# A hybrid decoder layer: small joint products placed one by one between the large ones, and two of seven sums formed by TensorE

## The chip, the cores and the metric

The kernel runs on one core of one Trainium2 chip. The metric is the device time of one execution in microseconds (us), as the median of several runs. The core has five engines with their own queues, each strictly in the order in which its instructions were issued: TensorE (PE, matmuls; PEld are its weight loads), VectorE (DVE), ScalarE (ACT), GpSimd (POOL) and SyncE (SP, which here only starts transfers). PE writes its results into PSUM, which has eight banks of 128 x 512 float32; DVE and ACT read it, POOL does not.

## What is computed

One layer on 1024 tokens of width 1024, all in float32:

```python
def _hybrid_layer(x, norm_g, w_in, ...):
    h = _rmsnorm(x, norm_g)
    p = h @ w_in                      # 1024 x 1024 times 1024 x 6656
    (u, v, z_a, x_b, b_g, c_g, z_b, x_c, z_c, g_a, g_b, g_c) = jnp.split(p, _split_points(), axis=-1)
    y_a = (_gmlp_branch(u, v, ln_g, ln_b, w_s, b_s) * jax.nn.silu(z_a)) @ w_pa
    y_b = (_shortconv_branch(x_b, b_g, c_g, conv_w, conv_b) * jax.nn.silu(z_b)) @ w_pb
    y_c = (_pool_branch(x_c, w_pool, pool_scale) * jax.nn.silu(z_c)) @ w_pc
    merged = jax.nn.sigmoid(g_a) * y_a + jax.nn.sigmoid(g_b) * y_b + jax.nn.sigmoid(g_c) * y_c
    return x + merged @ w_o
```

and a final RMSNorm over the result. The change lies in `h @ w_in`.

## The kernel before

There are three stages. The first (to 76 us) normalises and transposes x, forms its sums and does the columns of v. The middle stage (76 to 632 us) does the other 56 column tiles of `w_in`, two at a time: 28 pairs, `for p, (kind, j, _) in enumerate(pairs)`. The last one does the branch projections, the merge and the output product.

**Products.** A pair of column tiles (B, 2 x 2 blocks of weights) against the activations (A, 2 x 2 blocks) is done with seven block products instead of eight (Strassen's scheme in Winograd's form). `PRODUCTS` numbers them 0 to 6: A11·B11, A12·B21, S2·T2, S3·T3, S1·T1, A22·T4, S4·B22, with sums S of A and T of B. Each float32 operand is cut into a high and a low part, so `mm3` issues three matmuls for each of four 128-row blocks: 12 matmuls of 128 x 512 for one large product. The results are combined by seven sums: with P0 copied to `s1` by ACT, `o0` low half = P0 + P1, `u2` = P2 + s1, `u3` = P3 + u2, `o1` high half = P4 + u3, `u2` = P4 + u2, `o0` high half = P5 + u3, `o1` low half = P6 + u2. All are DVE adds; `block` does those that form a result and the activation behind them.

**Joint products.** From pair 2 on (`PLAIN = 2`), product 1 of an even pair and of the odd one behind it are taken together and done by the same scheme one level down, as seven small products of six matmuls of 128 x 256. `joint(d0, d1)` does all seven ahead of the even pair, in the order `SUB_ORDER`, with one ACT copy and seven DVE adds of 128 x 256 into two buffers `p2`; each pair then adds its `p2` to P0. So a large pair has six products from there on, (0, 2, 3, 4, 5, 6). Their A sums (`*_again`) are made once, in `cut_again`.

**Order.** `steps` lists all products in the order of the code. `product()` takes the next step, calls `ahead`, which prepares the weights (T sums, the cut into high and low by ACT and DVE or POOL) of up to six steps ahead and starts loads up to twelve ahead, and then issues the matmuls into a new PSUM bank. A framework places waits and buffers: tiles of one tag share a fixed number of buffers (PSUM 8; `raw` 4; `q` 6 for p2, s1, u2, u3 and others; `m` 5 for o0, o1 and the buffers of the branches; `wc` 18 for weights). When the program is built it also fixes each engine's order of instructions, which need not be that of the code.

**Kinds of pairs.** The order of kinds is g g g a g a g a g a, then four times b bz, then four times c g, then g g. Gates (g) get a sigmoid and are stored from ACT's queue. For each a pair, `spatial` loads `vr` during the pair before, `spatial_norm` scales it (eight DVE instructions, line 445, two POOL multiplications, a cut), `spatial_mm` uses it in the a pair, and `gate` runs in the pair behind (`late`). Behind a b pair, DVE runs a convolution of three passes; behind a c pair it runs `pooled`, a chain of up to five passes over 128 x 1024 and a cut.

Line 76 is the helper `tt` (every two-operand DVE or POOL instruction), lines 79 and 80 the cut, lines 83 to 85 `mm3`, line 546 the copy to `s1`.

Of the kernel before, what the change touches and what calls it, by code (L numbers as in the profile page):

```python
# [11 lines left out]
ALU = mybir.AluOpType  # L12

P = 128
# [9 lines left out]
HALF = 512  # L24
# [17 lines left out]

PRODUCTS = (("A11", "B11"), ("A12", "B21"), ("S2", "T2"), ("S3", "T3"),
            ("S1", "T1"), ("A22", "T4"), ("S4", "B22"))
BLOCKS = ("A11", "A12", "A22", "S1", "S2", "S3", "S4")
SUB_ORDER = (0, 2, 1, 3, 4, 5, 6)
PLAIN = 2
AHEAD = 6  # L50
RAW_AHEAD = 12
# [4 lines left out]
def hybrid_layer(ctx: ExitStack, tc: tile.TileContext, x, units, ws, wpool, small, rows, out):  # L56
    nc = tc.nc
# [8 lines left out]
    def slot(tag, name, shape, dtype=F32):  # L66
        return big.tile(list(shape), dtype, name=name, tag=tag, bufs=BUFS[tag])

    def bank(name, shape=(P, HALF)):
        return psum.tile(list(shape), F32, name=name, tag="ps")  # L70

    def tsl(i, n=P):
        return slice(i * n, (i + 1) * n)

    def tt(eng, o, a, b, op):
        eng.tensor_tensor(out=o, in0=a, in1=b, op=op)  # L76
# [2 lines left out]
        nc.scalar.copy(out=hi, in_=src)  # L79
        tt(eng or nc.vector, lo, src, hi.bitcast(F32), ALU.subtract)  # L80

    def mm3(ps, wh, wl, bh, bl, first, last):
        nc.tensor.matmul(ps, lhsT=wh, rhs=bh, start=first, stop=False)  # L83
        nc.tensor.matmul(ps, lhsT=wh, rhs=bl, start=False, stop=False)  # L84
        nc.tensor.matmul(ps, lhsT=wl, rhs=bh, start=False, stop=last)  # L85

    tmp = const.tile([P, 3, 3, NT], F32, name="tmp")

# [76 lines left out]
    hb = {}  # L165
# [95 lines left out]
    pairs = []  # L261
# [11 lines left out]


    steps = []
    for p in range(len(pairs)):
        if p < PLAIN:
            steps += [("n", p, r) for r in range(7)]
        else:
            if p % 2 == 0:  # L280
                steps += [("j", p, r) for r in SUB_ORDER]
            steps += [("n", p, r) for r in (0, 2, 3, 4, 5, 6)]
    NP = len(steps)

    raw, T, comb = {}, {}, {}
# [6 lines left out]
    def prep(n):  # L292
        kind, p, r = steps[n]
        name = PRODUCTS[r][1]
        u0, u1 = pairs[p][2]
        load_raw(u0)
        if kind == "n":
            load_raw(u1)
            b = {"B11": raw[u0][:, 0, :], "B21": raw[u0][:, 1, :], "B12": raw[u1][:, 0, :], "B22": raw[u1][:, 1, :]}
        else:  # L300
            v0 = pairs[p + 1][2][0]
            load_raw(v0)
            b = {"B11": raw[u0][:, 1, 0:256], "B21": raw[u0][:, 1, 256:], "B12": raw[v0][:, 1, 0:256],
                 "B22": raw[v0][:, 1, 256:]}

        def add(name, i0, i1, into=None):
            if kind == "n":
                t = bank(f"{name}_{kind}{p}")
            else:
                t = slot("T", f"{name}_{kind}{p}", (P, HALF)) if into is None else into  # L310
            if kind == "j" and into is None:
                T[kind, p, name, "rest"] = t[:, 256:]
                t = t[:, 0:256]
            tt(nc.vector if kind == "n" else nc.gpsimd, t, b[i0] if i0 in b else T[kind, p, i0], b[i1] if i1 in b else T[kind, p, i1], ALU.subtract)
            T[kind, p, name] = t

        if r == 2:
            add("T1", "B12", "B11")
            add("T2", "B22", "T1", T["j", p, "T1", "rest"] if kind == "j" else None)
        elif r == 3:  # L320
            add("T3", "B22", "B12")
        elif r == 5:
            add("T4", "B21", "T2", T["j", p, "T3", "rest"] if kind == "j" else None)
        if kind == "n":
            hi = slot("wc", f"ch{n}", (P, HALF), F32R)
            lo = slot("wc", f"cl{n}", (P, HALF), F32R)
            if name in b:
                split_to(hi, lo, b[name], nc.gpsimd)
            else:
                split_to(hi, lo, T[kind, p, name])  # L330
            comb[n] = (hi, lo)
        elif r == 0:
            hi = slot("wc", f"ch{n}", (P, HALF), F32R)
            lo = slot("wc", f"cl{n}", (P, HALF), F32R)
            split_to(hi, lo, raw[u0][:, 1, :])
            comb[n] = (hi[:, 0:256], lo[:, 0:256])
            comb[n + SUB_ORDER.index(1)] = (hi[:, 256:], lo[:, 256:])
        elif r > 1:
            w = slot("wc", f"cj{n}", (P, 2, 256), F32R)
            split_to(w[:, 0, :], w[:, 1, :], b[name] if name in b else T[kind, p, name])  # L340
            comb[n] = (w[:, 0, :], w[:, 1, :])
# [13 lines left out]
    at_step = [0]  # L355
    sub = {}

    def product():
        n = at_step[0]
        at_step[0] += 1  # L360
        ahead(n)
        kind, p, r = steps[n]
        wh, wl = comb.pop(n)
        if kind == "n":
            ah, al = hb[PRODUCTS[r][0]]
            ps = bank(f"p{n}")
        else:
            ah, al = sub[PRODUCTS[r][0]]
            ps = bank(f"p{n}", (P, 256))
        nk = KH if kind == "n" else KH // 2  # L370
        for k in range(nk):
            mm3(ps, wh[:, tsl(k)], wl[:, tsl(k)], ah[:, k, :], al[:, k, :], k == 0, k == nk - 1)
        return ps

    def cut_again(first):
# [21 lines left out]
            sub["S4"] = sub["A21"]  # L397
            split_to(*sub["S4"], sub["f"])

    def joint(d0, d1):  # L400

        lo, hi = slice(0, 256), slice(256, HALF)
        nc.scalar.copy(out=d0[:, lo], in_=product())
        tt(nc.vector, d1[:, lo], product(), d0[:, lo], ALU.add)
        tt(nc.vector, d0[:, lo], product(), d0[:, lo], ALU.add)
        tt(nc.vector, d0[:, hi], product(), d1[:, lo], ALU.add)
        ps = product()
        tt(nc.vector, d1[:, hi], ps, d0[:, hi], ALU.add)
        tt(nc.vector, d1[:, lo], ps, d1[:, lo], ALU.add)
        tt(nc.vector, d0[:, hi], product(), d0[:, hi], ALU.add)  # L410
        tt(nc.vector, d1[:, lo], product(), d1[:, lo], ALU.add)


    for n, i in enumerate(TOKENS):
# [8 lines left out]
    gates = [dram.tile([P, S], F32, name=f"gate{n}") for n in range(24)]  # L423
# [3 lines left out]
    def spatial(j):  # L427
        both = slot("q", f"wsr{j}", (P, 4, P))
        wsr, lnr = both[:, 0:2, :], both[:, 2:4, :]
        nc.scalar.dma_start(out=wsr, in_=ws[:, 2 * j:2 * j + 2, :])  # L430
        nc.gpsimd.affine_select(out=wsr, in_=wsr, pattern=[[0, 2], [1, P]], compare_op=ALU.is_ge, fill=0.0,
                                base=0, channel_multiplier=-1)
        wss = slot("q", f"wss{j}", (P, 2, 2 * P), F32R)
        src = wsr.rearrange("p g t -> p (g t)")
        split_to(wss[:, 0, :], wss[:, 1, :], src)
        for r in range(2):
            lo = r * CW + j * P
            nc.scalar.dma_start(out=lnr[:, r, :], in_=rows[0:1, lo:lo + P].broadcast_to([P, P]))
# [72 lines left out]
    lohalf, hihalf = slice(0, HALF), slice(HALF, S)  # L511
# [5 lines left out]
    for p, (kind, j, _) in enumerate(pairs):  # L517
        nxt = pairs[p + 1] if p + 1 < len(pairs) else (None, None)
        f0, f1 = FUNCS[kind]
        o0 = slot("m", f"o0_{p}", (P, S))  # L520
        o1 = slot("m", f"o1_{p}", (P, S))
# [12 lines left out]
            elif func:  # L534
                nc.scalar.activation(out=dst, in_=dst, func=func)

        if p >= PLAIN and p % 2 == 0:
            p2, p2_next = (slot("q", f"p2_{p + e}", (P, HALF)) for e in range(2))
            joint(p2, p2_next)
        elif p >= PLAIN:  # L540
            p2 = p2_next
        s1 = slot("q", f"s1_{p}", (P, HALF))
        u2 = slot("q", f"u2_{p}", (P, HALF))
        u3 = slot("q", f"u3_{p}", (P, HALF))
        ps = product()
        nc.scalar.copy(out=s1, in_=ps)
        if nxt[0] == "a":
            sp_next = spatial(nxt[1])
        if p < PLAIN:
            block(o0, lohalf, product(), s1, f0)  # L550
        else:
            block(o0, lohalf, ps, p2, f0)
        if p == PLAIN - 1:
            cut_again(False)
        tt(nc.vector, u2, product(), s1, ALU.add)
        tt(nc.vector, u3, product(), u2, ALU.add)
        if nxt[0] == "a":
            sp_next = spatial_norm(nxt[1], *sp_next)
        if p == 0:
            cut_again(True)  # L560
        ps = product()
        block(o1, hihalf, ps, u3, f1)
        tt(nc.vector, u2, ps, u2, ALU.add)
        block(o0, hihalf, product(), u3, f0)
        if kind == "a":
            st = spatial_mm(j, *sp)
        sp = sp_next
        if late is not None:
            late()
            late = None  # L570
        if kind == "g":
            nc.scalar.dma_start(out=gates[2 * j], in_=o0)
        block(o1, lohalf, product(), u2, f1)

        if kind == "g":
            nc.scalar.dma_start(out=gates[2 * j + 1], in_=o1)
# [131 lines left out]
    for b in range(3):  # L708
        for e, d in enumerate(ORDER):
            n = 8 * b + e  # L710
# [10 lines left out]
            wh, wl = wps.pop(n)  # L721
            py = [bank(f"py{n}_{h}") for h in range(2)]
            for c in range(CT):
                for w, s in ((wh, 0), (wh, 1), (wl, 0)):
                    for h in range(2):
                        nc.tensor.matmul(py[h], lhsT=w[:, tsl(c)], rhs=yt[b][h][s][:, c, :],  # L726
                                         start=c == 0 and w is wh and s == 0, stop=c == CT - 1 and w is wl)
# [188 lines left out]
```

## Time and profile before

| | |
|---|---|
| median of 3 runs | 864.05 us (864.03 to 864.22) |
| the profiled execution | 864.74 us |
| its span, first to last instruction | 863.0 us |
| mean granted TensorE clock | 0.984 of full speed |
| PE busy | 826.1 us (96%) |
| DVE busy | 661.5 us (77%) |
| ACT busy | 341.2 us (40%) |
| POOL busy | 373.5 us (43%) |

A line of a timeline or of a group names source line, engine, operation, "out<-in" by the program's tile names without numbers (`p` is a bank of a product, but also a `p2` buffer; `T_n` a T sum of a large product, `ch`/`cl` and `cj` cut weights, `o` a result, `u` one of u2 and u3, `s` is s1, `pl` and `pw` belong to `pooled`), and the shape. In brackets stands the idle time of the engine in front of the instruction and what ended it. Matmuls overlap: each takes 0.39 us from start to end at 512 columns, but the next starts before that.

### The profile page before, as it was taken

To read this page: it belongs to the slowest core of one execution; us is meant where nothing else is said; L and a number is where in the kernel's file an instruction comes from. 1 tells how busy PE (TensorE), PEld (TensorE's weight loads), DVE (VectorE), ACT (ScalarE), POOL (GpSimd) and SP (SyncE) were. 2 spreads that over 40 slices of the span, in tenths; PEclk is the share of its full clock that TensorE was granted. 3 is DMA by queue.
4 is the path that set the end of the run, shared out by engine and by line. 5 is a ranking of instruction groups with operands and counts; after the bars stand their busy time and mean duration, and the time that the engine had idled before them with its cause. 6 is when DMAs were issued, how large, how long until landed. Compare 5 with 4: busy or idle time off the path is not lost.

```text
span 863.0 us, 11355 instructions
## 1 busy us (share of the span) xinstructions
PE 826.1 (96%) x3950; PEld 694.5 (80%) x3950; DVE 661.5 (77%) x1102; ACT 341.2 (40%) x667; POOL 373.5 (43%) x347
## 2 busy tenths in 40 slices
PE   7999999898989999999999999999999999997993
PEld 6787888787878888888888888888888888775883
DVE  6867887878787878869686787879565735897995
ACT  4545444444444433323234453535342401343431
POOL 5743535646464624354351213141000352548874
PEclk8999999999999999999999999999999999999997
DMA  7412332323323212031121413323498553421044
GB/s 293 159 38 74 119 124 88 110 98 93 116 85 123 74 49 98 25 118 65 62 94 32 150 73 102 119 80 123 147 333 301 171 171 122 147 74 50 11 161 146
DMA packets 33880, 99.57 MB, mean 115 GB/s; under 512 B 3488, under 2 KB 9632, under 8 KB 33824
## 3 DMA queue, kind: packets, MB, share of 16 engines
q1 hardware_dynamic: 27920, 83.90, 28.2%
q10 hardware_dynamic: 5904, 14.96, 4.9%
q8 instruction: 31, 0.51, 0.2%
q14 instruction: 25, 0.20, 0.1%
HBM read 73.68 MB, written 25.17 MB: 115 GB/s over the span
## 4 chain that ended last, share of the span: by engine, by line
PE 78%; DVE 11%; DMA 3%; POOL 3%; issue 2%; ACT 1%; POOLq 0%; DVEq 0%; ACTq 0%
PE p L83 20%; PE p L85 20%; PE p L84 20%; PE py L726 10%; DVE al L76 3%; PE pv L85 2%; PE pv L83 2%; DVE rq L76 2%; PE pv L84 2%; POOL res L76 1%; DVE mg L76 1%; POOL S_a L76 1%; DVE vr L445 1%; DVE gt L76 1%; DMA out_dram<-res 1%
## 5 line engine op out<-in xcount | busy, mean ns | idle before, releaser
L76 POOL TENSOR_TENSOR cl<-raw,ch 128x512 fp32r<-128x512 f32 x58 | 79.8, 1378 | 230.7 <-ACT ch L79 105.3
L79 ACT CAST ch<-T_n 128x512 fp32r<-128x512 f32 x112 | 64.7, 587 | 116.7 <-PE p L84 61.3
L76 DVE TENSOR_TENSOR o<-p,u 128x512 f32<-128x512 f32 x84 | 57.7, 687 | 43.2 <-PE p L85 42.7
L76 DVE TENSOR_TENSOR cl<-T_n,ch 128x512 fp32r<-128x512 f32 x112 | 75.5, 679 | 7.2 <-ACT ch L79 6.8
L79 ACT CAST ch<-raw 128x512 fp32r<-128x512 f32 x71 | 43.7, 620 | 70.4 <-PE p L84 59.5
L76 DVE TENSOR_TENSOR u<-p,u 128x512 f32<-128x512 f32 x56 | 38.3, 683 | 10.6 <-PE p L85 9.6
L83 PE MATMUL p<-A11h,ch 128*128 128x512 f32 x112 | 44.3, 396 | 0.3 <-ACT ch L79 0.3
L85 PE MATMUL p<-A11h,cl 128*128 128x512 f32 x112 | 43.7, 390 | 0.6 <-POOL cl L76 0.6
L83 PE MATMUL p<-S4h,ch 128*128 128x512 f32 x112 | 43.9, 392 | 0.0
L84 PE MATMUL p<-A11l,ch 128*128 128x512 f32 x112 | 43.8, 391 | 0.0
L85 PE MATMUL p<-S4h,cl 128*128 128x512 f32 x112 | 43.6, 389 | 0.0
L84 PE MATMUL p<-S4l,ch 128*128 128x512 f32 x112 | 43.6, 389 | 0.0
L85 PE MATMUL p<-A22h,cl 128*128 128x512 f32 x112 | 43.6, 389 | 0.0
L83 PE MATMUL p<-S2h,ch 128*128 128x512 f32 x112 | 43.6, 389 | 0.0
L84 PE MATMUL p<-S2l,ch 128*128 128x512 f32 x112 | 43.6, 389 | 0.0
L85 PE MATMUL p<-S2h,cl 128*128 128x512 f32 x112 | 43.6, 389 | 0.0
L83 PE MATMUL p<-S3h,ch 128*128 128x512 f32 x112 | 43.6, 389 | 0.0
L84 PE MATMUL p<-S3l,ch 128*128 128x512 f32 x112 | 43.6, 389 | 0.0
L85 PE MATMUL p<-S3h,cl 128*128 128x512 f32 x112 | 43.6, 389 | 0.0
L83 PE MATMUL p<-S1h,ch 128*128 128x512 f32 x112 | 43.6, 389 | 0.0
L84 PE MATMUL p<-S1l,ch 128*128 128x512 f32 x112 | 43.6, 389 | 0.0
L85 PE MATMUL p<-S1h,cl 128*128 128x512 f32 x112 | 43.6, 389 | 0.0
(475 smaller groups left out, 2533.0 us busy)
## 6 DMA issues: line engine op xcount, KB each, us to landing
raw<-in_units_dram SPq DMA_DIRECT2D x56, 512.0 KB, 3.3
gate<-o ACTq DMA_DIRECT2D x24, 512.0 KB, 3.1
gt<-gate SPq DMA_DIRECT2D x24, 512.0 KB, 4.5
rawp<-in_units_dram SPq DMA_DIRECT2D x12, 512.0 KB, 3.6
yr<-y SPq DMA_DIRECT2D x12, 512.0 KB, 4.8
x<-in_x_dram SPq DMA_DIRECT2D x8, 512.0 KB, 6.7
y<-o SPq DMA_DIRECT2D x8, 512.0 KB, 2.6
rawo<-in_units_dram SPq DMA_DIRECT2D x8, 512.0 KB, 3.3
```

The costliest lines, as they stand in the source:

```text
L76: eng.tensor_tensor(out=o, in0=a, in1=b, op=op)
L79: nc.scalar.copy(out=hi, in_=src)
L83: nc.tensor.matmul(ps, lhsT=wh, rhs=bh, start=first, stop=False)
L84: nc.tensor.matmul(ps, lhsT=wh, rhs=bl, start=False, stop=False)
L85: nc.tensor.matmul(ps, lhsT=wl, rhs=bh, start=False, stop=last)
L445: nc.vector.tensor_scalar(out=vr[:, i, :], in0=vr[:, i, :], scalar1=mv[:, i, 0:1], scalar2=lr[:, i:i + 1], op0=ALU.subtract, op1=ALU.mult)
L726: nc.tensor.matmul(py[h], lhsT=w[:, tsl(c)], rhs=yt[b][h][s][:, c, :], start=c == 0 and w is wh and s == 0, stop=c == CT - 1 and w is wl)
```

## The change

Six things change.

1. The seven small products are no longer done in a row ahead of an even pair. `subs_behind` puts them behind large products: in the odd pair before, one behind product 3, two behind product 5, one behind product 6; in the even pair, one each behind products 0, 4 and 2. Their order becomes 0, 2, 1, 3, 5, 4, 6. `joint(q, r)` now does one of them; `then` is called behind each large product and does those that stand next in `steps`.
2. The large products go in the order 0, 4, 2, 3, 5, 6 (`ORDER_N`; pairs 0 and 1 have product 1 behind 0). T1 is formed for product 4.
3. Product 2 is accumulated onto the bank of product 0 (`px`) after `o0 <- P0 + p2` has read it. ACT copies P0+P2 to `u2`; `s1` is gone (pairs 0 and 1 also copy P0).
4. Product 6 is accumulated onto the bank of product 4 (`py_`) after `o1 <- P4 + u3` has read it; the second `u2` add is gone. In the same way the small product 6 goes onto the bank of the small product 4.
5. `spatial_norm` and `cut_again(True)` stand behind `o1 <- P4 + u3` instead of ahead of it.
6. The store of a gate's `o0` stands right behind its last half instead of behind the late work.

```diff
 BLOCKS = ("A11", "A12", "A22", "S1", "S2", "S3", "S4")
-SUB_ORDER = (0, 2, 1, 3, 4, 5, 6)
+ORDER_N = (0, 4, 2, 3, 5, 6)
+SUB_ORDER = (0, 2, 1, 3, 5, 4, 6)
+SUB_BEFORE = {3: 1, 5: 2, 6: 1}
+SUB_WITHIN = {0: 1, 4: 1, 2: 1}
...
     steps = []
+    subs = {p: list(SUB_ORDER) for p in range(PLAIN, len(pairs), 2)}
+    def subs_behind(p, r):
+        q = p + p % 2
+        at = SUB_BEFORE if p % 2 else SUB_WITHIN
+        return q, [subs[q].pop(0) for _ in range(at.get(r, 0))] if q in subs else []
     for p in range(len(pairs)):
-        if p < PLAIN:
-            steps += [("n", p, r) for r in range(7)]
-        else:
-            if p % 2 == 0:
-                steps += [("j", p, r) for r in SUB_ORDER]
-            steps += [("n", p, r) for r in (0, 2, 3, 4, 5, 6)]
+        for r in ((0, 1) + ORDER_N[1:] if p < PLAIN else ORDER_N):
+            steps.append(("n", p, r))
+            q, rs = subs_behind(p, r)
+            steps += [("j", q, e) for e in rs]
...
-        if r == 2:
+        if r == 4 and kind == "n":
             add("T1", "B12", "B11")
+        elif r == 2:
+            if kind == "j":
+                add("T1", "B12", "B11")
             add("T2", "B22", "T1", T["j", p, "T1", "rest"] if kind == "j" else None)
...
-    def product():
+    def product(want, onto=None, more=False):
...
+        ps = bank(f"p{n}", (P, HALF) if kind == "n" else (P, 256)) if onto is None else onto
         nk = KH if kind == "n" else KH // 2
         for k in range(nk):
-            mm3(ps, wh[:, tsl(k)], wl[:, tsl(k)], ah[:, k, :], al[:, k, :], k == 0, k == nk - 1)
+            mm3(ps, wh[:, tsl(k)], wl[:, tsl(k)], ah[:, k, :], al[:, k, :], k == 0 and onto is None,
+                k == nk - 1, more or onto is not None)
...
-    def joint(d0, d1):
+    def joint(q, r):
         lo, hi = slice(0, 256), slice(256, HALF)
-        nc.scalar.copy(out=d0[:, lo], in_=product())
-        tt(nc.vector, d1[:, lo], product(), d0[:, lo], ALU.add)
-        tt(nc.vector, d0[:, lo], product(), d0[:, lo], ALU.add)
-        tt(nc.vector, d0[:, hi], product(), d1[:, lo], ALU.add)
-        ps = product()
-        tt(nc.vector, d1[:, hi], ps, d0[:, hi], ALU.add)
-        tt(nc.vector, d1[:, lo], ps, d1[:, lo], ALU.add)
-        tt(nc.vector, d0[:, hi], product(), d0[:, hi], ALU.add)
-        tt(nc.vector, d1[:, lo], product(), d1[:, lo], ALU.add)
+        if r == 0:
+            for e in range(2):
+                both[q + e] = slot("q", f"p2_{q + e}", (P, HALF))
+        d0, d1 = both[q], both[q + 1]
+        if r == 4:
+            held[q] = product(("j", r), more=True)
+            tt(nc.vector, d1[:, hi], held[q], d1[:, hi], ALU.add)
+        elif r == 6:
+            tt(nc.vector, d1[:, lo], product(("j", r), held[q]), d1[:, lo], ALU.add)
+        elif r == 0:
+            nc.scalar.copy(out=d0[:, lo], in_=product(("j", r)))
+        else:
+            d, part = {2: (d1[:, lo], d0[:, lo]), 1: (d0[:, lo], d0[:, lo]), 3: (d1[:, hi], d1[:, lo]),
+                       5: (d0[:, hi], d1[:, hi])}[r]
+            tt(nc.vector, d, product(("j", r)), part, ALU.add)
...
-        s1 = slot("q", f"s1_{p}", (P, HALF))
...
-        ps = product()
-        nc.scalar.copy(out=s1, in_=ps)
+        px = product(("n", 0), more=True)
         if nxt[0] == "a":
             sp_next = spatial(nxt[1])
+        then(0)
         if p < PLAIN:
-            block(o0, lohalf, product(), s1, f0)
+            nc.scalar.copy(out=u2, in_=px)
+            block(o0, lohalf, product(("n", 1)), u2, f0)
...
         else:
-            block(o0, lohalf, ps, p2, f0)
...
-        tt(nc.vector, u2, product(), s1, ALU.add)
-        tt(nc.vector, u3, product(), u2, ALU.add)
-        if nxt[0] == "a":
-            sp_next = spatial_norm(nxt[1], *sp_next)
-        if p == 0:
-            cut_again(True)
-        ps = product()
-        block(o1, hihalf, ps, u3, f1)
-        tt(nc.vector, u2, ps, u2, ALU.add)
-        block(o0, hihalf, product(), u3, f0)
+            block(o0, lohalf, px, both[p], f0)
+        py_ = product(("n", 4), more=True)
+        then(4)
+        nc.scalar.copy(out=u2, in_=product(("n", 2), px))
+        then(2)
+        tt(nc.vector, u3, product(("n", 3)), u2, ALU.add)
+        block(o1, hihalf, py_, u3, f1)
+        then(3)
+        if p == 0:
+            cut_again(True)
+        if nxt[0] == "a":
+            sp_next = spatial_norm(nxt[1], *sp_next)
+        block(o0, hihalf, product(("n", 5)), u3, f0)
+        if kind == "g":
+            nc.scalar.dma_start(out=gates[2 * j], in_=o0)
+        then(5)
         if kind == "a":
             st = spatial_mm(j, *sp)
...
-        if kind == "g":
-            nc.scalar.dma_start(out=gates[2 * j], in_=o0)
-        block(o1, lohalf, product(), u2, f1)
+        block(o1, lohalf, product(("n", 6), py_), u2, f1)
+        then(6)
```

## Rows read from the trace of the kernel before

**Rows 1.** The page: busy time, share of the span and instructions of each engine

```profile
PE 826.1 (96%) x3950; PEld 694.5 (80%) x3950; DVE 661.5 (77%) x1102; ACT 341.2 (40%) x667; POOL 373.5 (43%) x347
```

**Rows 2.** Waits of PE, 76 to 632 us: in total, times, longest

```profile
PE p L83 <- DVE cl L76: 5.6, 3, 1.9
PE p L83 <- DVE o L76: 2.1, 3, 0.7
```

**Rows 3.** Windows: length, busy (instructions) of PE, PEld, DVE, ACT, POOL, clock, DMA

```profile
115.10:120.10 5.00, 5.00 (x43) 4.98 (x42) 5.00 (x12) 3.41 (x7) 0.00 (x0) 1.00 0.50 185
154.10:162.20 8.10, 5.56 (x44) 5.11 (x43) 7.08 (x16) 2.62 (x5) 4.77 (x3) 1.00 0.08 25
197.10:206.40 9.30, 6.75 (x44) 6.31 (x43) 8.25 (x19) 3.73 (x7) 5.00 (x3) 0.85 0.09 26
241.70:250.90 9.20, 6.66 (x43) 6.24 (x42) 8.26 (x18) 3.64 (x7) 5.00 (x3) 0.84 0.07 17
...
251.00:632.00 381.00, 381.00 (x1866) 323.31 (x1866) 298.03 (x480) 154.01 (x276) 131.97 (x107) 1.00 0.27 95
```

**Rows 4.** Timeline of DVE in the joint group at 154 us: start, us, instruction

```profile
155.59 0.54 DVE L445 TENSOR_SCALAR vr<-vr,mv,lr 128x128 f32<-128x128 f32 x1 [1.02 <-DMA vr<-v_dram]
...
157.76 2.31 DVE L445 TENSOR_SCALAR vr<-vr,mv,lr 128x128 f32<-128x128 f32 x5
```

**Rows 5.** Timeline of PE in the same group

```profile
157.89 0.39 PE L83 MATMUL p<-S1h_again,cj 128*128 128x256 f32 x1 [0.69 <-DVE o L76]
...
160.72 0.39 PE L83 MATMUL p<-A12h,cj 128*128 128x256 f32 x1 [1.85 <-DVE cl L76]
```

**Rows 6.** Groups by form, 76 to 632 us: count, busy us, mean ns, idle before

```profile
L76 DVE TENSOR_TENSOR u<-p,u 128x512 f32<-128x512 f32 x56 | 38.3, 683 | 10.6 <-PE p L85 9.6 <-POOL T_j L76 0.9
...
L76 DVE TENSOR_TENSOR p<-p,p 128x256 f32<-128x256 f32 x91 | 34.6, 410 | 0.0
...
L76 DVE TENSOR_TENSOR u<-p,s 128x512 f32<-128x512 f32 x28 | 19.2, 685 | 10.7 <-PE p L85 10.7
L76 DVE TENSOR_TENSOR o<-p,p 128x512 f32<-128x512 f32 x26 | 17.7, 682 | 5.0 <-ACT s L546 4.8
L546 ACT COPY s<-p 128x512 f32<-128x512 f32 x28 | 16.3, 581 | 0.4 <-PE p L85 0.4
```

**Rows 7.** Timeline of PE in pair 0, from product 1 on

```profile
79.75 0.39 PE L83 MATMUL p<-A12h,ch 128*128 128x512 f32 x1
...
80.21 0.39 PE L83 MATMUL p<-S2h,ch 128*128 128x512 f32 x1
...
82.70 0.39 PE L83 MATMUL p<-A12h,ch 128*128 128x512 f32 x1
```

**Rows 8.** Timeline of PE: first matmul of product 0 in pairs 11, 21, 23, 25

```profile
308.41 0.39 PE L83 MATMUL p<-A11h,ch 128*128 128x512 f32 x1
498.43 0.39 PE L83 MATMUL p<-A11h,ch 128*128 128x512 f32 x1
537.49 0.39 PE L83 MATMUL p<-A11h,ch 128*128 128x512 f32 x1
576.55 0.39 PE L83 MATMUL p<-A11h,ch 128*128 128x512 f32 x1
```

**Rows 9.** Timeline of DVE: the add `o0 <- P0 + p2` of these pairs, and neighbours

```profile
313.98 0.68 DVE L76 TENSOR_TENSOR o<-p,p 128x512 f32<-128x512 f32 x1
504.76 0.68 DVE L76 TENSOR_TENSOR o<-p,p 128x512 f32<-128x512 f32 x1
545.62 0.68 DVE L76 TENSOR_TENSOR o<-p,p 128x512 f32<-128x512 f32 x1
583.17 0.68 DVE L76 TENSOR_TENSOR u<-p,s 128x512 f32<-128x512 f32 x1
585.77 1.23 DVE L76 TENSOR_TENSOR pw<-pl,ph 128x1024 fp32r<-128x1024 f32 x1 [0.17 <-ACT ph L79]
586.91 0.68 DVE L76 TENSOR_TENSOR o<-p,p 128x512 f32<-128x512 f32 x1
```

More of the change, by code (lines that the diff above doesn't have):

```diff
@@ L80, in split_to, with mm3 @@
         tt(eng or nc.vector, lo, src, hi.bitcast(F32), ALU.subtract)
[L82 to L85, printed above, removed]
+    def mm3(ps, wh, wl, bh, bl, first, last, shared=False):
+        nc.tensor.matmul(ps, lhsT=wh, rhs=bh, start=first, stop=False, skip_group_check=shared)
+        nc.tensor.matmul(ps, lhsT=wh, rhs=bl, start=False, stop=False, skip_group_check=shared)
+        nc.tensor.matmul(ps, lhsT=wl, rhs=bh, start=False, stop=last, skip_group_check=shared)
     tmp = const.tile([P, 3, 3, NT], F32, name="tmp")
@@ L336, in prep @@
             comb[n] = (hi[:, 0:256], lo[:, 0:256])
-            comb[n + SUB_ORDER.index(1)] = (hi[:, 256:], lo[:, 256:])
+            comb[steps.index(("j", p, 1))] = (hi[:, 256:], lo[:, 256:])
         elif r > 1:
@@ L362, in product @@
         kind, p, r = steps[n]
+        assert (kind, r) == want
         wh, wl = comb.pop(n)
[L364 to L369, printed above, removed]
+        ah, al = (hb if kind == "n" else sub)[PRODUCTS[r][0]]
+        ps = bank(f"p{n}", (P, HALF) if kind == "n" else (P, 256)) if onto is None else onto
         nk = KH if kind == "n" else KH // 2
         for k in range(nk):
-            mm3(ps, wh[:, tsl(k)], wl[:, tsl(k)], ah[:, k, :], al[:, k, :], k == 0, k == nk - 1)
+            mm3(ps, wh[:, tsl(k)], wl[:, tsl(k)], ah[:, k, :], al[:, k, :], k == 0 and onto is None,
+                k == nk - 1, more or onto is not None)
         return ps
@@ L398, in cut_again @@
             split_to(*sub["S4"], sub["f"])
-    def joint(d0, d1):
+    both, held = {}, {}
+    def joint(q, r):
         lo, hi = slice(0, 256), slice(256, HALF)
-        nc.scalar.copy(out=d0[:, lo], in_=product())
-        tt(nc.vector, d1[:, lo], product(), d0[:, lo], ALU.add)
-        tt(nc.vector, d0[:, lo], product(), d0[:, lo], ALU.add)
-        tt(nc.vector, d0[:, hi], product(), d1[:, lo], ALU.add)
-        ps = product()
-        tt(nc.vector, d1[:, hi], ps, d0[:, hi], ALU.add)
-        tt(nc.vector, d1[:, lo], ps, d1[:, lo], ALU.add)
-        tt(nc.vector, d0[:, hi], product(), d0[:, hi], ALU.add)
-        tt(nc.vector, d1[:, lo], product(), d1[:, lo], ALU.add)
+        if r == 0:
[13 more added lines that the diff above has]
+            tt(nc.vector, d, product(("j", r)), part, ALU.add)
     for n, i in enumerate(TOKENS):
@@ L535, in block, with then @@
                 nc.scalar.activation(out=dst, in_=dst, func=func)
[L537 to L541, printed above, removed]
-        s1 = slot("q", f"s1_{p}", (P, HALF))
+        def then(r):
+            while at_step[0] < NP and steps[at_step[0]][0] == "j":
+                joint(steps[at_step[0]][1], steps[at_step[0]][2])
         u2 = slot("q", f"u2_{p}", (P, HALF))
         u3 = slot("q", f"u3_{p}", (P, HALF))
-        ps = product()
-        nc.scalar.copy(out=s1, in_=ps)
+        px = product(("n", 0), more=True)
         if nxt[0] == "a":
             sp_next = spatial(nxt[1])
+        then(0)
         if p < PLAIN:
-            block(o0, lohalf, product(), s1, f0)
-        else:
-            block(o0, lohalf, ps, p2, f0)
-        if p == PLAIN - 1:
-            cut_again(False)
-        tt(nc.vector, u2, product(), s1, ALU.add)
-        tt(nc.vector, u3, product(), u2, ALU.add)
+            nc.scalar.copy(out=u2, in_=px)
+            block(o0, lohalf, product(("n", 1)), u2, f0)
+            if p == PLAIN - 1:
+                cut_again(False)
+        else:
+            block(o0, lohalf, px, both[p], f0)
[8 more added lines that the diff above has]
+            cut_again(True)
         if nxt[0] == "a":
             sp_next = spatial_norm(nxt[1], *sp_next)
-        if p == 0:
-            cut_again(True)
-        ps = product()
-        block(o1, hihalf, ps, u3, f1)
-        tt(nc.vector, u2, ps, u2, ALU.add)
-        block(o0, hihalf, product(), u3, f0)
+        block(o0, hihalf, product(("n", 5)), u3, f0)
+        if kind == "g":
+            nc.scalar.dma_start(out=gates[2 * j], in_=o0)
+        then(5)
         if kind == "a":
```

## The prediction

> **What bounds the kernel now.** I read the page first: TensorE (PE) is busy for 826.1 of 863.0 us, VectorE (DVE) for 661.5 [rows 1]. That alone says "PE-bound", so the next question is where PE is *not* busy, and only the middle stage (76 to 632 us, the 28 pairs) is touched by the change. The waits of PE there are few: three on a DVE subtraction, three on a DVE add [rows 2]. The windows show where: from 251 us to 632 us PE is busy for 381.00 of 381.00 us at clock 1.00, whereas three of the thirteen groups of small joint products have holes [rows 3]. A clean group takes 5.0 us from its first small product to the large one behind it; the groups at 154, 197 and 242 us take 8.1, 9.3 and 9.2. In each PE idles 2.54 or 2.55 us, and in the last two the granted clock is below 1.00 (0.85 and 0.84 of the window; part of it at the 1.2 GHz level) behind the idle time. So what the change can win is 3.1 + 4.3 + 4.2 = 11.6 us, 1.3% of the span. Everything else that it takes from DVE has no place on the path.
>
> Why those three? DVE sits 1.02 us in front of its queue's first `vr` scaling, waiting for a load, and then does five more in one go (2.31 us) [rows 4]. Meanwhile seven small products come in 5 us, each wanting a PSUM bank and an add; PE then stops first behind an add and then behind a subtraction that reads a bank [rows 5]: the banks are all waiting for DVE.
>
> **The change, part by part.**
> *Sums on TensorE.* Per pair the adds `u2 = P2 + s1` and `u2 = P4 + u2` go: 28 of 0.685 us and half of the 56 of 0.683 us; per joint group one of 0.410 us goes, 13 in all [rows 6]. That is 19.2 + 19.1 + 5.3 = 43.6 us of DVE, off the path while PE has no gap: worth nothing by itself outside the three groups. PE runs as many matmuls of the same shapes as before, so its own work costs 0. The ACT copy of P0 (0.581 us [rows 6]) becomes a copy of P0+P2; two copies more in pairs 0 and 1, beside PE work: 0.
>
> *Small products spread.* Seven in a row become runs of one or two. A run of one or two asks for as many banks and adds in the 2.7 us of the large product next to it, instead of seven in 5.0 us; the demand that filled the banks in [rows 5] is gone. I take all 11.6 us as won, and 0 as the other end. Next late is DVE's wait for `vr` itself: it is still there (1.02 us), see the second rival.
>
> *Order inside a pair* (0, 4, 2, 3, 5, 6). T1 is formed at the same second place as before, T2 one place later; both are DVE adds off the path, 0. Holding P0 and P4 in banks longer takes one or two more of the eight, while T1 and T2 are held for one product less each: I set these against each other. The new argument of `mm3` issues nothing.
>
> *New wait one: product 2 goes onto the bank that the add `o0 <- P0 + p2` reads.* Its first matmul waits for that add, and behind it in PE's queue wait all later products. A large product is 12 matmuls of 0.227 us (two take 79.75 to 80.21 [rows 7]), 2.72 us. In an odd pair only product 4 stands between, so product 2 is due 24 × 0.227 = 5.44 us after product 0 starts; in an even pair two small ones more, 6.9 us. Before, nobody waited for this add, and the trace shows when it came. After a pooling pair (odd pairs 19, 21, 23, 25) it comes behind the pooling chain (in pair 25 right behind its last pass, `pw` at 585.77 [rows 9]): product 0 starts at 498.43, 537.49 and 576.55 [rows 8], so product 2 would be due at 503.87, 542.93 and 581.99; the adds end at 504.76 + 0.68 = 505.44, 546.30 and 587.60 [rows 9]. Lateness 1.6, 3.4 and 5.6 us (pair 19: none). After a convolution pair (11, 13, 15, 17) 308.41 + 5.44 = 313.85 against 313.98 + 0.68 = 314.66: 0.8 us, four times alike. The other odd pairs and the even ones have room. Upper end: 1.6 + 3.4 + 5.6 + 4 × 0.8 = 13.8 us; lower end 0.
>
> Which value? At the four convolution pairs the add had to come behind ACT's copy of the same bank (4.8 us of its idle time over the run are ACT's [rows 6]), and that copy is gone: 0. At pair 25 the `u2` and `u3` adds stood between (0.6 us each by their starts, `u2` at 583.17 ahead of `o0` at 586.91 [rows 9]); those come later now, so 5.6 becomes 4.4. The order on PE is fixed when the program is built, and not strictly by the code: at 79.75 two matmuls of A12 are issued, then ten of S2, then A12 again [rows 7]. So I expect one other ready product, 2.72 us, to be put in front of the waiting one. That leaves 0, 0.7 and 1.7 us: 2.4 us. Without it, 9.4.
> The Trainium skill ("TensorE: Matmul & The Clock Gate", Part 2) says that matmuls themselves stay in program order on the chip and only weight loads are pulled ahead. By that the queue cannot help itself, and the sum for these pairs would be 9.4 us if the issue order isn't changed beforehand; the interleaving in [rows 7] can then only be an issue order.
>
> *New wait two: product 6 goes onto the bank of P4*, read by `o1 <- P4 + u3`. The two adds (0.68 each) follow product 3, and product 5 (2.72 us) runs meanwhile: 1.2 us to spare in even pairs, 3.3 in odd ones, where three small products lie between. `spatial_norm` (8 DVE scalings, 2 POOL products, a cast, a subtraction; no DMA) is moved behind this add, so it stands in front of the next pair's work rather than of this add: 0. The 8 scalings still share DVE with preparations that have six steps of lead.
>
> *Moves on queues.* The store of `o0` on ACT's queue goes ahead of the late work, past two ACT casts of `spatial_mm`: it frees a buffer sooner; 0. `cut_again(True)` comes one product later, and its results are due one large product earlier, in pair 1 instead of behind it; its inputs are ready all along: 0. `p2` buffers are taken half a pair earlier, one `s1` buffer is gone: 0, at worst an ACT copy is late by a POOL multiplication.
>
> **The sum.** 863.0 − 11.6 + 2.4 = 853.8 us of span. The profiled execution took 864.74 us, 1.74 more than its span, and the median of the runs is 0.69 below it: 853.8 + 1.74 − 0.69 = 854.9 us.
>
> **The rivals.**
> *A, the forecast, 0.58.* Its own range: 851.5 (no new wait, and the slow restart behind two stalls gone too) to 863.0 (the three pooling pairs at 10.6 us).
> *B, the `vr` burst still reaches PE, 0.14.* For: DVE's wait for the load is untouched by the change. Against: the deadline is now 6.9 us behind product 0 of an even pair, and what has to happen takes product 0, one small product (0.72) and two adds (0.41 + 0.69), 4.7 us. 1.02 + 2.31 = 3.3 us of delay overruns these 2.2 us by 1.1, three times: 858.3 us.
> *C, spreading does not remove the cause, 0.10.* The stalls follow the load and not the bunch, and come at other products: won and lost cancel, 863 to 866 us, 864.5 as the middle.
> *D, the readers of P0 set PE's pace, 0.18, on the other side.* All of 13.8 us is paid, and the two longest stalls cost clock as in [rows 3] (9.3 − 8.1 = 1.2 us each): 863.0 − 11.6 + 13.8 + 2.4 = 867.6 of span, 868.7 us. It decides from 13.3 us of new waits on (11.6 + 1.7). For: the lateness stands in the trace as it is. Against: it was free then, so nothing drew it forward.
> The Trainium skill ("PSUM — Partial Sum Buffer", the summary of rules) advises to read PSUM in a different bank from the one TensorE writes, and to guard by bank. This change does the opposite on purpose; by that rule D is the case to fear, and the trace of before can't show it, as no bank there is written again after a read.
>
> **How the numbers follow.** A measurement of this kernel can tell about 0.2% (1.7 us) from no change. Faster: A and B, 0.72. Same: most of C, 0.08. Slower: D and the rest of C, 0.20. The range goes from A's lower end through B and into C, 851.5 to 865.0, and leaves out D and the rest of C, some 0.2.
>
> **What will show it.** Right if the windows of PE between 150 and 252 us are full, DVE's busy time is down by about 44 us, and the clock stays at 1.00. New wait one shows as idle time in front of the first S2h matmul of pairs 21, 23 and 25, put down to the `o0` add; D is right if that idle time is over 10 us in sum. B shows as idle time next to `vr` rows. The forecast is wrong if PE waits in pairs 11 to 17, or if idle time appears in front of S4h (new wait two).

## The result and the profile after

The changed kernel is slower: 879.37 us median of four runs (878.41 to 881.47) against 864.13 us beside it, a ratio of 1.0174 (95% interval 1.0151 to 1.0198). 854.9 us was forecast, in a range of 851.5 to 865.0. The profiled run took 879.07 us, its span 877.3.

The page of the kernel after, busy time of each engine (beside [rows 1]):

```profile
PE 831.0 (95%) x3950; PEld 693.7 (79%) x3950; DVE 628.5 (72%) x1033; ACT 343.4 (39%) x671; POOL 382.0 (44%) x347
```

DVE has 69 instructions less and is busy for 33.0 us less; PE has as many as before and is busy for 4.9 us more. The matmuls are the same, so that points to a lower clock; where the rest of the loss is, the page doesn't say.

The stage of the 28 pairs was 556.0 us long and is now 567.9 (76.0 to 643.9); what follows it gained another 2.4 us, 1.8 of it behind the last matmul, which I didn't trace to an edit. So the question is the middle stage, and what PE waits for there. Kernel after, waits of PE, 76 to 644 us (total, times, longest; L83 is now the line of DVE's adds, L90 to L92 those of the matmuls, L429 ACT's copy of the first small product, L578 its copy of P0+P2):

```profile
PE p L90 <- DVE o L83: 11.8, 5, 3.5
PE p L90 <- ACT p L429: 1.3, 3, 0.4
PE pp L90 <- ACT u L578: 1.1, 2, 0.7
```

The waits of [rows 2] are gone, and a larger one stands there: matmuls that wait for a DVE add into an `o` buffer; four of the five, 11.6 of the 11.8 us, stand at the first matmul of product 2. That is new wait one of the prediction, product 2 onto the bank that `o0 <- P0 + p2` reads. But it isn't where I put it. Windows of the kernel after, from product 0 of pairs 2, 4, 6, 8 and 10 to the small product behind product 2 (columns as in [rows 3]):

```profile
118.40:131.30 12.90, 10.15 (x50) 8.18 (x49) 10.22 (x15) 4.01 (x7) 8.62 (x5) 1.00 0.40 126
160.80:175.70 14.90, 11.36 (x50) 9.34 (x49) 10.16 (x17) 4.20 (x8) 11.12 (x7) 0.89 0.21 60
206.10:220.10 14.00, 11.30 (x50) 9.32 (x50) 9.40 (x17) 3.87 (x7) 10.31 (x7) 0.88 0.20 63
250.50:264.60 14.10, 11.31 (x51) 9.29 (x51) 9.38 (x17) 3.87 (x7) 10.18 (x7) 0.88 0.19 60
295.00:304.60 9.60, 9.60 (x50) 8.15 (x49) 5.48 (x8) 2.95 (x5) 7.46 (x5) 1.00 0.30 104
```

The last line is a clean pair: 9.6 us, PE full. The four above do the same PE work and take 3.3, 5.3, 4.4 and 4.5 us longer, 17.5 in all. By the second column 11.8 of it are idle time (length less PE's busy time) and 5.7 longer busy time (10.15, 11.36, 11.30 and 11.31 against 9.60), 5.2 of that in the three pairs whose granted clock is 0.88 or 0.89. These are the even pairs ahead of a spatial pair ("a"), the place where the preparation of its branch, `spatial` and `spatial_norm`, is queued on DVE and POOL. The balance of the stage: −11.6 (the three stalls of [rows 3], gone) + 17.5 + 6.0 = +11.9. The 6.0 are what is left when the others are taken off. Most of it lies in pairs 11 to 26. Windows from product 0 of pair 11 to product 0 of pair 27, kernel before, then kernel after:

```profile
308.41:615.61 307.20, 307.20 (x1514) 261.21 (x1513) 244.94 (x396) 123.51 (x222) 102.48 (x83) 1.00 0.25 87
311.67:624.01 312.34, 309.67 (x1515) 261.32 (x1514) 231.83 (x358) 124.19 (x222) 108.01 (x83) 1.00 0.24 85
```

These pairs take 5.1 us more, at full clock, 2.7 of it idle time: six short stops of 0.3 to 0.7 us, among them those of the second and third line of the waits (1.3 + 1.1). The other 0.9 us of the 6.0 isn't placed.

Why is the add late? DVE in pair 4, whose product 0 starts at 160.82 and whose product 2 is due at 167.74, 0.12 behind the start of the last small matmul in front of it (start, length, instruction; in brackets the idle time in front):

```profile
161.56 1.90 DVE L467 TENSOR_SCALAR vr<-vr,mv,lr 128x128 f32<-128x128 f32 x4 [1.59 <-DMA vr<-v_dram]
163.39 0.68 DVE L83 TENSOR_TENSOR o<-p,u 128x512 f32<-128x512 f32 x1
163.99 2.20 DVE L467 TENSOR_SCALAR vr<-vr,mv,lr 128x128 f32<-128x128 f32 x4
166.10 0.68 DVE L83 TENSOR_TENSOR cl<-T_n,ch 128x512 fp32r<-128x512 f32 x1
...
167.63 0.68 DVE L83 TENSOR_TENSOR T_n<-raw,raw 128x512 f32<-128x512 f32 x1
168.24 0.41 DVE L83 TENSOR_TENSOR p<-p,p 128x256 f32<-128x256 f32 x1
168.57 2.22 DVE L83 TENSOR_TENSOR wss<-wsr,wss 128x256 fp32r<-128x256 f32 x1
170.72 0.68 DVE L83 TENSOR_TENSOR o<-p,p 128x512 f32<-128x512 f32 x1
```

The add is the last line. P0 has long been there; `p2` gets its last part from the small add at 168.24, which is late for the same reason. DVE comes to the add of P0 at 170.72 because it works off its queue in order: 1.59 us of waiting for the `vr` load, eight scalings (1.90 + 2.20), some adds and subtractions, and 2.22 us for a subtraction of 256 columns that with the same shape (`p<-p,p`, the line above it, with one input in PSUM) takes 0.41. (In the code `spatial_norm` stands behind `o1 <- P4 + u3`, point 5 of the change; in DVE's rows its scalings stand ahead of the same pair's add of P0 all the same.) POOL and PE of the same moments:

```profile
167.57 2.94 POOL L83 TENSOR_TENSOR vr<-vr,wsr 128x1024 f32<-128x1024 f32 x1 [0.77 <-DVE p L83]
```

```profile
167.38 0.28 PE L90 MATMUL p<-S1h_again,cj 128*128 128x256 f32 x1
171.45 0.80 PE L90 MATMUL p<-S2h,ch 128*128 128x512 f32 x1 [3.54 <-DVE o L83]
172.89 0.63 PE L90 MATMUL p<-S2h,ch 128*128 128x512 f32 x1
```

`wss` ends at 170.79, 0.28 us after POOL's multiplication (170.51); in pair 2 it ends at 124.21, 0.28 us after POOL's (123.93). There another subtraction of this kind, `cj<-raw,cj`, takes 1.65 us just before. And PE stands still for 3.54 us with product 2 at the head of its queue, then takes 1.44 us for three matmuls (171.45 to 172.89) that take 0.68 at the full clock.

The Trainium skill ("SBUF — State Buffer", Who interferes with whom) says that a DVE instruction with two SBUF inputs and a GpSimd one that reads SBUF exclude each other, the second waiting for the whole of the first. `wss <- wsr, wss` has two such inputs, and its two ends agree with the rule.

### The profile page after: what moved, and what is told of

The parts are those of the page before. It is cut to its first block, busy times and chain, and to the rows that moved or that the text cites. A ratio compares the mean times of both kernels' runs of the same rounds, so it can differ in the third digit from the quotient of the medians.

```text
span 877.3 us, 11162 instructions
## 1 busy us (share of the span) xinstructions
PE 831.0 (95%) x3950; PEld 693.7 (79%) x3950; DVE 628.5 (72%) x1033; ACT 343.4 (39%) x671; POOL 382.0 (44%) x347
## 4 chain that ended last, share of the span: by engine, by line
PE 74%; DVE 11%; DMA 6%; POOL 5%; issue 2%; ACT 2%; POOLq 0%; DVEq 0%; SPq 0%; ACTq 0%
PE p L90 19%; PE p L91 18%; PE p L92 18%; PE py L751 10%; DMA rawo<-in_units_dram 1%; DVE rq L83 1%; DVE vr L467 1%; POOL S_a L83 1%; DMA x<-in_x_dram 1%; POOL res L83 1%; PE pv L92 1%; DVE wss L83 1%; PE pv L90 1%; PE pv L91 1%; PE po L90 1%
## 5 line engine op out<-in xcount | busy, mean ns | idle before, releaser
L83 POOL TENSOR_TENSOR cl<-raw,ch 128x512 fp32r<-128x512 f32 x58 | 82.3, 1421 | 162.5 <-PE p L92 59.2
L83 DVE TENSOR_TENSOR cl<-T_n,ch 128x512 fp32r<-128x512 f32 x112 | 76.2, 682 | 51.4 <-PE p L91 44.9
L83 DVE TENSOR_TENSOR o<-p,u 128x512 f32<-128x512 f32 x86 | 58.2, 684 | 24.1 <-PE p L92 23.8
L90 PE MATMUL p<-S2h,ch 128*128 128x512 f32 x112 | 46.4, 414 | 12.0 <-DVE o L83 11.6
L83 DVE TENSOR_TENSOR cj<-T_j,cj 128x256 fp32r<-128x256 f32 x52 | 33.3, 642 | 31.9 <-ACT cj L86 31.9
L86 ACT CAST cj<-T_j 128x256 fp32r<-128x256 f32 x52 | 21.1, 406 | 65.5 <-PE p L91 54.6
L92 PE MATMUL p<-S2h,cl 128*128 128x512 f32 x112 | 45.1, 402 | 0.0
L557 ACT ACTIVATE o<-o 128x512 f32<-128x512 f32 x48 | 30.0, 631 | 37.9 <-DVE o L83 37.7
L90 PE MATMUL p<-A11h,ch 128*128 128x512 f32 x112 | 44.3, 396 | 0.3 <-ACT ch L86 0.3
L92 PE MATMUL p<-A11h,cl 128*128 128x512 f32 x112 | 43.8, 391 | 0.6 <-POOL cl L83 0.6
L90 PE MATMUL p<-A22h,ch 128*128 128x512 f32 x112 | 43.7, 391 | 0.0
L91 PE MATMUL p<-A22l,ch 128*128 128x512 f32 x112 | 43.7, 391 | 0.0
L90 PE MATMUL p<-S3h,ch 128*128 128x512 f32 x112 | 43.7, 391 | 0.0
L90 PE MATMUL p<-S1h,ch 128*128 128x512 f32 x112 | 43.7, 391 | 0.0
L91 PE MATMUL p<-S4l,ch 128*128 128x512 f32 x112 | 43.6, 389 | 0.0
L90 PE MATMUL p<-S4h,ch 128*128 128x512 f32 x112 | 43.6, 389 | 0.0
```

## The experiments

Theory: product 2's reuse of a bank that DVE reads turns DVE's delays (late load, scalings, the stretched subtraction) into PE's. Rivals: the holding of two banks through a pair leaves too few for the rest; the spreading itself; any one of DVE's delays alone. Ratios are against the kernel before, run beside each. No run takes back points 2, 5 and 6 of the change (the order of the products and the moves), so "spreading" and "the sums" each stand for their part together with these.

| label | spread | product 2 on P0 | product 6 on P4 | small sum | us | ratio |
|---|---|---|---|---|---|---|
| (after) | yes | yes | yes | yes | 879.37 | 1.0174 [1.0151, 1.0198] |
| e2_spread_only | yes | no | no | no | 854.17 | 0.9868 [0.9852, 0.9884] |
| e3_sums_only | no | yes | yes | yes | 877.59 | 1.0137 [1.0122, 1.0152] |
| e1_no_px | yes | no | yes | yes | 855.79 | 0.9887 [0.9872, 0.9902] |
| e8_py_only | yes | no | yes | no | 853.42 | 0.9860 [0.9843, 0.9876] |
| e4_px_copied | yes | yes, add reads a copy | yes | yes | 866.05 | 1.0014 [1.0002, 1.0025] |
| e5_no_scaling | yes | yes | yes | yes | 865.10 | 0.9990 [0.9976, 1.0004] |
| e6_wss_on_pool | yes | yes | yes | yes | 866.10 | 1.0009 [0.9993, 1.0026] |
| e7_both_off | yes | yes | yes | yes | 860.67 | 0.9942 [0.9922, 0.9962] |

**e1_no_px: product 2 gets its own bank.** Edit against the kernel after:

```diff
-        px = product(("n", 0), more=True)
+        s1 = slot("q", f"s1_{p}", (P, HALF))
+        px = product(("n", 0))
+        nc.scalar.copy(out=s1, in_=px)
...
-        nc.scalar.copy(out=u2, in_=product(("n", 2), px))
+        tt(nc.vector, u2, product(("n", 2)), s1, ALU.add)
```

> The changed kernel with one sum taken back: product 2 goes into a bank of its own, ACT copies P0 to s1 and DVE forms u2 = P2 + s1, as before the change. The spread and the sum on the bank of P4 stay. Theory 1 (the wait of product 2 for the DVE add that reads P0 carries the DVE delays of the spatial pairs to TensorE): the four waits in front of S2h in pairs 2, 4, 6, 8 (12.2 us) and the half clock behind them (4.8 us) go, 879.4 - 17.0 = about 862.4 us. Rival 2 (the spread itself costs: banks, preparation, small products beside large ones): stays at 876 to 880 us.

855.79 us, faster than expected. This one sum costs 879.37 − 855.79 = 23.6 us, more than the 17.5 read from the windows: pairs 11 to 26 lose their stops too, and take 307.9 us instead of 312.3. Waits of PE, e1, 76 to 632 us, DVE's line:

```profile
PE p L90 <- DVE p L83: 1.0, 1, 1.0
```

One wait is left, in pair 2: the small product 6 onto the bank of the small product 4, the same construction in small.

**e2_spread_only: all sums back on DVE.** Edit: as in e1, and also

```diff
-        py_ = product(("n", 4), more=True)
+        py_ = product(("n", 4))
...
+        tt(nc.vector, u2, py_, u2, ALU.add)
...
-        block(o1, lohalf, product(("n", 6), py_), u2, f1)
+        block(o1, lohalf, product(("n", 6)), u2, f1)
...
-            held[q] = product(("j", r), more=True)
+            held[q] = product(("j", r))
+            tt(nc.vector, d1[:, lo], held[q], d1[:, lo], ALU.add)
...
-            tt(nc.vector, d1[:, lo], product(("j", r), held[q]), d1[:, lo], ALU.add)
+            tt(nc.vector, d1[:, lo], product(("j", r)), d1[:, lo], ALU.add)
```

> The spread alone: the order of the changed kernel, all seven sums on DVE (product 2, product 6 and the small product 6 in banks of their own). Theory 1: the 43.6 us of DVE adds that come back lie beside TensorE, so as with product 2 alone in its own bank, 862 us, give or take 3; DVE busy up by about 44 us. Rival 2: 876 to 880 us or more, as the spread is all there.

854.17 us, 5 us below the expected range: the rest of the loss wasn't the spread's. It is the time of the forecast, from one half of the change. The page:

```profile
PE 822.4 (96%) x3950; PEld 690.3 (81%) x3950; DVE 660.4 (77%) x1102; ACT 340.0 (40%) x667; POOL 380.4 (45%) x347
```

DVE is busy for 660.4 us here and for 661.5 before; still the kernel is 1.3% faster. So the gain doesn't come from DVE's total load. (Against the kernel after, DVE is busy for 31.9 us more, not 44.) Of waits the middle stage has only the two at its start, which e8 shows below.

**e3_sums_only: the small products in a row as before, the sums on TensorE.**

```diff
+        if p >= PLAIN and p % 2 == 0:
+            steps += [("j", p, e) for e in SUB_ORDER]
         for r in ((0, 1) + ORDER_N[1:] if p < PLAIN else ORDER_N):
             steps.append(("n", p, r))
-            q, rs = subs_behind(p, r)
-            steps += [("j", q, e) for e in rs]
```

> The sums alone: the seven small products in a row ahead of the even pair as before the change, large products in the new order with the sums on the banks of P0 and P4. Theory 1: the waits in front of S2h in pairs 2, 4, 6, 8 stay, and the bunch of small products is back: 872 to 890 us. Rival 2: the cost goes with the spread, 852 to 862 us.

877.59 us, in the expected range, but by another way. Waits of PE, e3, 76 to 632 us:

```profile
PE p L90 <- ACT p L429: 6.4, 7, 2.0
PE p L90 <- DVE T_n L83: 3.6, 6, 2.3
PE p L90 <- DVE p L83: 1.0, 1, 1.0
```

No wait for an `o` add: the stall of product 2 isn't there. PE stops inside the rows of small products instead, the longest at 161.29 (2.32 us), 208.20 and 252.10 (2.03 each), put down to a DVE subtraction and to ACT's copy of the first small product (L429), and the clock is 0.66 in the window from 160 to 166 us and 0.77 in the next six. Pairs 11 to 26 take 314.5 us, 7.3 more than before. So the two halves of the change don't add up: spreading wins 11.5 us without the sums (865.7 to 854.2) and nothing clear with them (877.6 and 879.4, with intervals of the ratio that touch); the sums cost 12 us without spreading (865.7 to 877.6) and 25 with it (854.2 to 879.4).

**e8_py_only: spread, and the one sum on P4's bank alone.** e1's edit, and of e2's the lines on `held`.

> The spread, and of the sums only that on the bank of P4 (product 2 and the small product 6 in banks of their own). Theory 1: nothing waits for DVE at a short deadline any more: the 1.0 us wait of the small product 6 in pair 2 that was left in the run without the sum on P0 goes, 854 to 855 us, no different from the spread alone (854.2), as the 19 us of DVE adds saved lie beside TensorE. Rival: the sum on P4 has a price of its own or frees DVE for something, over 855.5 or under 853 us.

853.42 us, the best of all, 1.4% below the kernel before, and 0.6 below the expected range. From e1 to e8 only the small sum goes; their times are 2.4 us apart. Against e2, e8 has the sum on P4's bank in addition: DVE is busy for 640.8 us instead of 660.4, and the two times are 0.75 us apart, with intervals of the ratio that overlap. In e8's middle stage PE has only the two waits that stand at its start:

```profile
PE p L92 <- POOL cl L83: 0.6, 1, 0.6
PE p L90 <- ACT ch L86: 0.3, 1, 0.3
```

**e4_px_copied: is it the add's place, or the bank?** ACT copies P0 out at once, the add reads the copy, and product 2 still goes onto P0's bank.

```diff
+        s1 = slot("q", f"s1_{p}", (P, HALF))
         px = product(("n", 0), more=True)
+        nc.scalar.copy(out=s1, in_=px)
...
-            block(o0, lohalf, px, both[p], f0)
+            block(o0, lohalf, s1, both[p], f0)
```

> The changed kernel, but ACT copies P0 to a buffer as soon as it is there, and the add of o0 reads that copy: product 2 then waits for an ACT copy (0.58 us) and no longer for DVE. One ACT copy of 0.58 us more per pair (28 in all, 16 us of ACT). Theory 1: the S2h waits shrink to what ACT is late, under 1 us each: 862 to 867 us. Rival 2: 876 to 880 us.

866.05 us: 13.3 us back, not all. The wait in front of product 2 is gone; its successor in PE's queue takes it over. Waits of PE, e4, 76 to 632 us:

```profile
PE p L90 <- DVE p L83: 6.5, 4, 2.0
```

They stand at 128.40, 169.80, 213.71 and 257.66, in the same four pairs, in front of the small product 6, which goes onto the bank that DVE's add of the small product 4 reads. The granted clock is below 1.00 behind the last three. DVE is still late, and the next place where PE writes a bank that DVE reads in between pays for it. The rival "two banks held" falls here: in e4 P0's bank is held as in the changed kernel, and pairs 11 to 26 take 308.0 us, as in e1, without a stop.

**e5, e6, e7: which of DVE's delays?** e5 leaves out the eight scalings per spatial pair (the `for` loop in `spatial_norm`), and with them DVE's wait for the `vr` load; e6 puts the subtraction `wss` on POOL; e7 does both.

```diff
-        for i in range(NT):
-            nc.vector.tensor_scalar(out=vr[:, i, :], in0=vr[:, i, :], scalar1=mv[:, i, 0:1], scalar2=lr[:, i:i + 1],
-                                    op0=ALU.subtract, op1=ALU.mult)
```

```diff
-        split_to(wss[:, 0, :], wss[:, 1, :], src)
+        split_to(wss[:, 0, :], wss[:, 1, :], src, nc.gpsimd)
```

> The changed kernel without the eight DVE scalings of vr in each of the four spatial pairs (this leaves the layer norm of branch A out; the two POOL multiplications stay). Theory 1a (the add that reads P0 stands in DVE's queue behind the wait for the load of vr and the scalings, 1.6 + 4.1 us): the waits in front of S2h in pairs 4, 6, 8 (9.5 us) and their half clock (4.8 us) go, that of pair 2 gets shorter: 862 to 866 us. Rival 1b (it is wss, the 128x256 subtraction that takes 2.2 us instead of 0.4 while POOL multiplies): the waits shrink little, 872 to 879 us.

> The changed kernel with the four wss subtractions (128x256, 2.2 to 2.6 us on DVE) on POOL. Theory 1a: the waits in front of S2h lose 2.2 us at most and remain in pairs 4, 6, 8: 868 to 874 us. Rival 1b: they go, 862 to 866 us.

> The changed kernel without the eight scalings (the layer norm of branch A left out) and with the wss subtractions on POOL. Either theory: with both gone DVE reads P0 in time, the waits in front of S2h are under 1 us in sum and the half clock is gone: 858 to 863 us. If it stays over 868 us, something else of the change holds the add back.

e5 865.10 us, e6 866.10, e7 860.67. e5 and e7 lie where they were expected, e6 below theory 1a's range and 0.1 above 1b's. Waits of PE in the middle stage, the line for DVE's add, e5 and then e6 (e7 has no such line):

```profile
PE p L90 <- DVE o L83: 3.7, 4, 1.6
```

```profile
PE p L90 <- DVE o L83: 4.6, 4, 1.5
```

11.8 us become 3.7 or 4.6, and 0 with both: both causes make the add late, and neither does it alone. Taking away either one brings 13 to 14 us, 7 to 8 of them idle time and some 5 the clock, which is at 1.00 behind all of these shorter stalls; taking away both brings 18.7. The late load and the scalings aren't told apart. e7 is still 4.9 us above e1, and its pairs 11 to 26 take 312.3 us as in the kernel after (e1: 307.9). That is what the wait of product 2 for DVE's add costs there, and not the held bank, as e4 shows: short stops, of which 2.4 us are in e7's list:

```profile
PE p L90 <- ACT p L429: 1.3, 3, 0.4
PE pp L90 <- ACT u L575: 1.1, 2, 0.7
```

## Why the prediction was wrong

**The win was right.** 11.6 us for spreading; e2, which has that and none of the sums, gains 865.7 − 854.2 = 11.5, and its middle stage has none of the stalls of [rows 3]. The reading of [rows 3] to [rows 5] held: seven banks and adds in 5 us were the trouble, not DVE's load.

**The failed step** is new wait one, put at 2.4 us in all, and in it the sentence "The other odd pairs and the even ones have room". Pairs 2, 4, 6 and 8, even ones that had "room", pay 17.5 us. The pairs that I had priced do not stop for DVE's add, as other products are put in front of product 2; this much was foreseen. Pooling pair 25, DVE's add and PE's first matmul of products 3, 5 and 2:

```profile
597.43 0.68 DVE L83 TENSOR_TENSOR o<-p,p 128x512 f32<-128x512 f32 x1
```

```profile
592.04 0.39 PE L90 MATMUL p<-S3h,ch 128*128 128x512 f32 x1
...
595.47 0.40 PE L90 MATMUL p<-A22h,ch 128*128 128x512 f32 x1
...
599.65 0.40 PE L90 MATMUL p<-S2h,ch 128*128 128x512 f32 x1
```

The large products with S3 and A22 (3 and 5) are put in front of product 2, which finds the add done at 598.11; I had expected one. In the convolution pairs 13, 15 and 17 these two stand in front of product 2 as well. But it isn't free: product 2 comes late, the ACT copy of its bank with it, and PE stops for short times behind ACT (0.42 us at 369.24, 407.76 and 446.28, 0.40 at 563.12, 0.68 at 603.23). Pairs 11 to 26 take 5.1 us more than before, 4.4 more than in e1 and e4, where product 2 doesn't wait for DVE. So new wait one came to 17.5 + 4.4 us or so, and not 2.4; and the four short waits in pairs 12 to 17, though none is put down to this add, were by the prediction's last part a sign that it is wrong.

**Rival B named half of the mechanism and got the size wrong.** It said that the `vr` burst reaches PE because "1.02 + 2.31 = 3.3 us of delay overruns these 2.2 us by 1.1, three times". Measured against the rows of pair 4: the wait for the load is 1.59 us and not 1.02; the scalings are eight, 4.10 us, and not the five of 2.31 that [rows 4] show in one go; and `wss`, 2.22 us, is missing altogether. It stood in the groups by form of the kernel before, a plain subtraction of 256 columns with 1.87 us as its mean, beside the 0.41 of another with the same shape:

```profile
L76 DVE TENSOR_TENSOR wss<-wsr,wss 128x256 fp32r<-128x256 f32 x4 | 7.5, 1866 | 0.7 <-ACT wss L79 0.7
...
L76 DVE TENSOR_TENSOR cj<-raw,cj 128x256 fp32r<-128x256 f32 x13 | 5.4, 414 | 0.0
```

Nor were the places three but four: ahead of pair 2 the group in [rows 3] (115.1) is clean, so I left it out, but DVE has the same preparation to do there. And B charged no clock, 5.2 us. Smaller slips of the sums: the terms of B's 4.7 us add up to 4.5, and those of new wait two leave 1.4 and 3.5 us to spare and not 1.2 and 3.3; no choice hangs on them.

**D** was the right outcome (868.7 us, decided from 13.3 us of new waits on) at the wrong pairs, and still 10.7 us short. Its own sign, over 10 us of idle time in front of S2h in pairs 21, 23 and 25, did not come: there is none there.

**Step "sums on TensorE": half right.** The sum on P4's bank is free, as said (new wait two never shows; e8). The adds taken from DVE are worth nothing by themselves, as said. DVE's relief was put at 43.6 us and is 33.0: the 69 adds are gone, but other instructions became longer. The largest of these are two subtractions (905 to 1187 ns mean for `T_n<-raw,raw`, 571 to 642 for `cj<-T_j,cj`), while `T_n<-raw` became shorter. Why isn't shown.

**The step on `spatial_norm`.** That it "stands in front of the next pair's work rather than of this add: 0" was wrong: in pairs 4, 6 and 8 its scalings stand in DVE's queue ahead of the same pair's add of P0, the first of its adds. "Holding P0 and P4 in banks longer" was rightly put at 0: e4 holds them as long and pays nothing for it in pairs 11 to 26.

**Open.** Why PE has other products in front of product 2 in pooling and convolution pairs and none in pairs 2 to 8 can be argued: the order is fixed when the program is built, where the length of DVE's chain is known, but not a load that lands late or a subtraction that POOL holds up. The traces fit this: in e1, e4 and e8, where product 2 needs no DVE add, it stands directly behind product 4 again in pair 25 (S1, S2, S3), and products 3 and 5 come after it. No run was made to test it.

## What to carry to other kernels

A sum formed by PE in a bank that another engine reads in between saves an add and buys a deadline: from then on that engine's whole queue in front of the reader is on PE's path, so list it instruction by instruction at each place, with the longest duration seen and not the mean, and do it for the places with much slack too. Such a sum is free where the bank is read by work that is due anyway (product 6 on P4), and here it cost most where a late load and a stretched instruction stood ahead of the reader. Where the order is fixed in advance, a deadline that is seen then can cost too, by the order that evades it (4.4 us here). And two edits that each look separable may not be: spreading was worth 11.5 us without the sums and nothing clear beside them.

## What the runs showed of the hardware

- A DVE subtraction of 128x256 with both inputs in SBUF, 0.41 us in the mean of its like in the kernel before, takes 2.22 and 2.62 us when POOL multiplies beside it, and ends 0.28 us after POOL does. With it on POOL (e6) the kernel is 13 us faster. One row looks otherwise: `T_n<-raw,raw`, with two SBUF inputs too, takes 0.68 us at 167.63, while POOL's row begins at 167.57. But there POOL seems to have been the one that waited: in pairs 4, 6 and 8 its multiplication ends 2.20, 2.21 and 2.20 us behind the end of that subtraction, whenever its row begins, and the row lasts 2.94, 2.69 and 2.56 us where the shortest of its kind lasts 2.39.
- PE's clock after a stall isn't told by the stall's length alone: behind 2.56 us of idle time (pair 2 of after) it stayed at full speed, behind 2.70 and 2.79 (pairs 6 and 8) the window has 0.88, and in e4 one behind 1.97 us (169.80 to 174) has 0.59. In [rows 3] stalls of 2.54 or 2.55 us in all go with 1.00 once and with 0.85 and 0.84. In e3, behind 2.03 us at 208.20 the six us from 210 on have 0.74, and behind 2.03 us at 252.10 those from 252 and 258 on have 1.00:

```profile
210.00:216.00 6.00, 6.00 (x21) 4.75 (x21) 3.22 (x7) 1.62 (x4) 6.00 (x4) 0.74 0.35 100
...
252.00:258.00 6.00, 5.90 (x29) 5.02 (x30) 5.55 (x11) 2.69 (x6) 5.92 (x4) 1.00 0.56 132
258.00:264.00 6.00, 6.00 (x31) 5.08 (x30) 5.09 (x7) 1.66 (x3) 6.00 (x4) 1.00 0.27 89
```
